# Seven products on the second of four slices, sixteen transfers in place of sixteen ScalarE copies, and weight halves split four ahead

## The chip, the cores and the metric

The kernel runs on one core of a Trainium2 chip. The metric is the device time of one execution in microseconds (us). Of the core's engines, TensorE (PE) multiplies, VectorE (DVE) and ScalarE (ACT) do the elementwise work, and SyncE (SP) issues transfers; each takes its own instructions strictly in order, and they wait for each other by semaphores.

## The reference

Two decoder layers on 256 tokens of width 2048. The change touches only the last two lines of a layer, the SwiGLU part, and what surrounds it:

```python
for l in range(DEPTH):                       # 2 layers
    h = rms_norm(x, attn_norm[l])
    z = h @ w_in[l]                          # 2048 -> 5632, split among three mixers
    ...
    x = x + mix @ w_out[l]                   # 2048 -> 2048
    h = rms_norm(x, ffn_norm[l])
    x = x + (jax.nn.silu(h @ w_gate[l]) * (h @ w_up[l])) @ w_down[l]   # 2048 -> 5632 -> 2048
return rms_norm(x, final_norm)
```

All is float32. The kernel gets float32 accuracy by splitting each operand into a rounded high part and a low remainder and adding three products: high by high, high by low, low by high.

## The kernel before

**Weights.** All weights come as blocks of 512 by 512 (1 MB), in the order of use, into four buffers `wf` (`load_weights`, SP, line 136). Each block is split in two halves (`split_weights`): ACT writes the high part `wh` (line 159), DVE the low part `wl` (line 160); five buffers hold split halves. `ahead(3)`, called at the start of each half's products, splits the half that is used three later. So a half's copy on ACT waits until PE has left the half used five before it.

**Products.** `products` (lines 207 to 209) is six matmuls of 128x512. A plain half is used for both token tiles, twelve matmuls. For one of the four 512-deep slices of gate and up, the one numbered `SEVEN`, the eight products (gate and up, two halves, two token tiles) are replaced by seven on sums (`seven`, `seven_products`): seven singles of six matmuls. In four of the seven, DVE first adds two halves in place (line 154), then ACT copies, then DVE makes the remainder.

**A block f.** Each layer has eleven blocks f of 512 columns of gate and up, in three parts of 4, 4 and 3. In a block PE works through the slices of the 2048-deep sum: first the seven singles of slice 0, then slices 1 to 3, twelve plain halves; 42 + 144 = 186 matmuls. Then DVE and ACT make `mid` = silu(gate) * up (lines 784 to 789). After each part comes its down projection with the `mid` of its blocks, transposed, as the stationary operand: `thd` and `tld`.

**The transposing of a mid.** `block_transposed` puts tasks into a list, and `step()`, called after each half used, runs the next one: DVE transposes 32x32 blocks within partitions (line 434, `btd`); ACT moves the 16 pieces between groups of 32 partitions (line 442, `bod`), four per task; ACT and DVE split the result in two tasks (lines 492 and 493). These seven tasks fall into the uses that follow, which are the seven singles of the next block, or the first halves of the down projection. `later(..., gap=n)` keeps a task at least n steps behind the one before.

**Order.** A scheduler places the instructions on each engine, near the order in which they are written. SP's instructions, loads and others, run in one row, and each transfer uses one of eight completion semaphores in turn, so that the ninth waits for the first to have landed.

Of the kernel before, what the change touches and what calls it, by code (L numbers as in the profile page):

```python
# [11 lines left out]
F32 = mybir.dt.float32  # L12
F32R = mybir.dt.float32r
I32 = mybir.dt.int32
AF = mybir.ActivationFunctionType
ALU = mybir.AluOpType
AX = mybir.AxisListType

P = 128
D = 2048  # L20
S = 256
NT = S // P
L = 2
CW = 512
NX = D // CW
# [28 lines left out]
def trunk_kernel(ctx: ExitStack, tc, x, positions, w_in, gmlp_ln_g, gmlp_ln_b,  # L54
# [8 lines left out]
    nc = tc.nc  # L63
# [9 lines left out]
    def blk(shape, name, dt=F32):  # L73
        return bpool.tile(shape, dt, tag="blk", name=name)
# [7 lines left out]

    PAIR = [(n, k) for n in range(2) for k in range(NX - 1)] + [(n, NX - 1) for n in range(2)]
    PARTS = [list(range(0, 4)), list(range(4, 8)), list(range(8, NF))]
    SEVEN = 0
    wsrc = []
    jobs = []

    def wblock(w, k, c):
        return w[c, k].rearrange("p (k c) -> p k c", k=4)  # L90
# [13 lines left out]
    for l in range(L):  # L104
# [10 lines left out]
        for hv in PARTS:  # L115
            for f in hv:
                for k in range(NX):
                    if k == SEVEN:
                        seven(wblock(w_gate[l], k, f), wblock(w_up[l], k, f))
# [45 lines left out]
    def ahead(n):  # L165

        j = min(state["use"] + n, len(jobs) - 1)
        split_weights(j + 1)
        load_weights(jobs[state["use"]][0] + 4)
# [6 lines left out]
    def later(fn, key=None, wait=0, gap=0):  # L176

        pending.append((fn, key, clock["now"] + wait, gap))
# [13 lines left out]
    def need(key):  # L192
        while key not in done:
            run_one()
# [16 lines left out]
    def block(operand, h, t):  # L211
        return [[x[:, 2 * h + k, t * P:(t + 1) * P] for k in range(2)] for x in operand]

    def weight_tile(acc, operand, first, last):
        for h in range(2):
            ahead(3)
            for t in range(NT):
                products(acc[t], *block(operand, h, t), state["use"], first[t] and h == 0, last and h == 1)
            whalf.pop(state["use"])
            state["use"] += 1  # L220
            step()

    def seven_products(dst, operand, sums):

        sh, sl = sums
        S = [[[x[:, n, k] for k in range(2)] for x in (sh, sl)] for n in range(4)]
        lhs = [block(operand, 0, 0), S[0], S[2], S[3], S[1], block(operand, 1, 0), block(operand, 1, 1)]
        for (acc, first, last), x in zip(dst, lhs):
            ahead(3)
            products(acc, *x, state["use"], first, last)  # L230
            whalf.pop(state["use"])
            state["use"] += 1
            step()
# [57 lines left out]
    stat = {}  # L291
    for c in range(NX):
        xt = blk([P, 4, S], f"xt{c}")
        th, tl = blk([P, 4, S], f"tha0_{c}", F32R), blk([P, 4, S], f"tla0_{c}", F32R)
# [131 lines left out]
    def transpose_later(src, name, per=1, wait=0):  # L426


        b = blk([P, NT, CW], f"bt{name}")
        o = blk([P, 4, S], f"bo{name}")  # L430

        def blocks():
            for t in range(NT):
                nc.vector.transpose(b[:, t], src[:, t])  # L434

        def moves(a0):
            for a in range(a0, a0 + per):
                for q in range(4):
                    s_ = b[32 * a:32 * a + 32].rearrange("p t (k q i) -> p t k q i", k=4, q=4)[:, :, :, q, :]
                    d_ = o[32 * q:32 * q + 32].rearrange("p k (t a i) -> p t k a i", t=NT, a=4)[:, :, :, a, :]  # L440
                    if q < 2 or name.startswith("d_"):
                        nc.scalar.copy(d_, s_)  # L442
                    else:
                        nc.vector.tensor_copy(d_, s_)

        later(blocks, wait=wait)
        for a in range(0, 4, per):
            later(lambda a=a: moves(a))
        return o

    def block_transposed(src, dst, key, gcol, per=1, wait=0):

        nm = "_".join(map(str, key))
        th, tl = blk([P, 4, S], f"th{nm}", F32R), blk([P, 4, S], f"tl{nm}", F32R)
        dst[key] = (th, tl)
        o = transpose_later(src, nm, per=per, wait=wait)
        for h in range(2):
            later(lambda h=h: evac_split(o[:, 2 * h:2 * h + 2], th, tl, 2 * h, gcol), key if h else None)
        return o

    def block_sums(stat, key, gcol):

# [85 lines left out]
    for l in range(L):  # L548
# [193 lines left out]
        stat = {}  # L742
# [3 lines left out]
        def projected(c, acc):  # L746
            add_residual(acc, c)
            norm_chunk(c, ssq, 32 + 16 * l, stat, f"f{l}", c == SEVEN)

# [5 lines left out]
        fkeys = [(f"f{l}", c) for c in range(NX)]  # L755
        rf = None
        for hi, hv in enumerate(PARTS):
            mids = {}
            for f in hv:
                P1, P5, P7, P6 = (trp.tile([P, CW], F32, tag="tr", name=f"p{n}_{f}") for n in (1, 5, 7, 6))  # L760
                C = [[accp.tile([P, CW], F32, tag="acc", name=f"c{f}_{n}{t}") for t in range(NT)] for n in range(2)]
                need(fkeys[SEVEN])
                need((f"f{l}", "sums"))
                alone = (True, True)
                seven_products([(P1, *alone), (P5, *alone), (P7, *alone), (C[1][0], True, False),
                                (P6, *alone), (C[0][0], True, False), (C[0][1], True, False)],
                               stat[fkeys[SEVEN]], stat["sums"])
                if rf is None:
                    rf = token_rstd(ssq, "rf")
                sg, mid = blk([P, NT, CW], "sg"), blk([P, NT, CW], "mid")  # L770

                nc.scalar.copy(sg[:, 0], P1)
                nc.vector.tensor_tensor(mid[:, 0], sg[:, 0], P6, op=ALU.add)
                nc.vector.tensor_tensor(sg[:, 1], mid[:, 0], P7, op=ALU.add)
                nc.vector.tensor_tensor(mid[:, 0], P5, mid[:, 0], op=ALU.subtract)
                nc.vector.tensor_tensor(mid[:, 1], P5, sg[:, 1], op=ALU.subtract)
                rest = [k for k in range(NX) if k != SEVEN]
                for k in rest:
                    need(fkeys[k])
                    for n in range(2):  # L780
                        weight_tile(C[n], stat[fkeys[k]], [False, n == 1 and k == rest[0]], k == rest[-1])
                        for t in range(NT if k == rest[-1] else 0):
                            if n == 0:
                                nc.vector.tensor_tensor(sg[:, t], sg[:, t], C[0][t], op=ALU.add)
                                nc.scalar.activation(sg[:, t], sg[:, t], AF.Silu, scale=rf[:, t:t + 1])
                            else:
                                nc.vector.tensor_tensor(mid[:, t], mid[:, t], C[1][t], op=ALU.add)  # L787
                for t in range(NT):
                    nc.vector.scalar_tensor_tensor(mid[:, t], mid[:, t], rf[:, t:t + 1], sg[:, t],  # L789
                                                   op0=ALU.mult, op1=ALU.mult)  # L790
                block_transposed(mid, mids, ("d", l, f), None)
            lastpart = hi == len(PARTS) - 1
            if lastpart:
                stat2 = {}
                ssq2 = spool.tile([P, NT, NX], F32, tag="ssq", name=f"ssq_n{l}")
                if l == L - 1:
                    fin = [blk([P, 2, CW], f"fin{h}") for h in range(2)]
                    for h in range(2):
                        nc.sync.dma_start(out=fin[h], in_=final_norm[h * 2 * CW:(h + 1) * 2 * CW].rearrange(
                            "(c n) -> c n", c=2).partition_broadcast(P))  # L800
                    xf = [[blk([P, 2, CW], f"xf{t}{h}") for h in range(2)] for t in range(NT)]
            for c in range(NX):
                last = l == L - 1 and lastpart and c == NX - 1
                acc = chunk(mids, [("d", l, f) for f in hv], 2 if last else 0)
                if last:
                    break
                add_residual(acc, c)
                if lastpart:
                    if l + 1 < L:
                        norm_chunk(c, ssq2, 16 * (l + 1), stat2, f"a{l + 1}")  # L810
                    else:
                        sum_squares(c, ssq2)
                        for t in range(NT):
                            nc.gpsimd.tensor_tensor(xf[t][c // 2][:, c % 2], xs[:, t, c * CW:(c + 1) * CW],
                                                    fin[c // 2][:, c % 2], op=ALU.mult)
        stat, ssq = stat2, ssq2
# [3 lines left out]
    ov = out[0].rearrange("(t p) d -> p t d", p=P)  # L820
    c = NX - 1
    for t in range(NT):
# [9 lines left out]
        for h in range(2):  # L832
            o = xf[t][h]
# [47 lines left out]
```

## Time and profile before

| | us |
|---|---|
| median of 3 runs | 2214.27 (2212.69 to 2215.53) |
| profiled execution | 2215.22 |
| its span, first to last instruction | 2213.5 |
| PE busy | 2132.7 (96%) |
| DVE busy | 1594.2 (72%) |
| ACT busy | 1269.1 (57%) |
| 16 DMA engines, mean busy share | 52.4% |

Matmuls overlap in a pipeline, so that a matmul's own duration (389 ns) is not the time that it costs; that is the distance from one start to the next. An engine's idle time counts only where PE, which is busy 96% of the span, is made to wait by it.

### The profile page before, as it was taken

What the parts mean: (1) busy time and instruction counts of PE and PEld (TensorE: products, weight loads), DVE (VectorE), ACT (ScalarE), POOL (GpSimd) and SP (SyncE); (2) the same over time, 40 slices, a digit from 0 to 9 for tenths busy, and PEclk for the clock granted to TensorE, in tenths of its full rate; (3) what the DMA queues carried; (4) which work ended last, traced back from release to release, by engine and by line L of the source; (5) the groups of instructions that cost most, each with busy time, mean ns of one, the idle gap of its engine ahead of it and who ended that gap; (6) DMA issues with size and microseconds to landing.
All of it is one profiled execution on the core that took longest, in us unless ns stands there. A gap on an engine that the chain in (4) does not pass through costs nothing.

```text
span 2213.5 us, 24728 instructions
## 1 busy us (share of the span) xinstructions
PE 2132.7 (96%) x9256; PEld 1736.2 (78%) x9256; DVE 1594.2 (72%) x1970; ACT 1269.1 (57%) x1849; POOL 176.6 (8%) x177
## 2 busy tenths in 40 slices
PE   9999999999999999999999999999899998999898
PEld 7888888777887778877788888887688877888676
DVE  6886788776567765676877768887765777657764
ACT  6565476556445564456756645765663466534663
POOL 6212400000000000000011024000000000000002
PEclk9999999999999999999999999999999999999999
DMA  8654555445554465545554554644465445654463
GB/s 308 226 190 167 195 202 197 171 152 209 191 191 170 152 212 207 190 152 207 177 215 174 193 186 171 220 179 152 170 226 194 171 152 191 219 198 152 165 235 114
DMA packets 62949, 417.44 MB, mean 189 GB/s; under 512 B 7535, under 2 KB 8047, under 8 KB 14189
## 3 DMA queue, kind: packets, MB, share of 16 engines
q1 hardware_dynamic: 62828, 415.86, 52.4%
q8 instruction: 72, 1.18, 0.2%
q14 instruction: 49, 0.39, 0.1%
HBM read 411.65 MB, written 2.10 MB: 187 GB/s over the span
## 4 chain that ended last, share of the span: by engine, by line
PE 77%; DVE 8%; ACT 7%; POOL 4%; issue 3%; DMA 0%; SPq 0%; ACTq 0%; POOLq 0%; DVEq 0%
PE acc L208 14%; PE acc L209 14%; PE acc L207 14%; PE c L207 11%; PE c L208 11%; PE c L209 11%; ACT wh L159 4%; DVE wl L160 3%; ACT bod L442 2%; DVE mid L789 1%; DVE btd L434 1%; DVE mid L787 1%; PE p L208 1%; POOL rtmp L332 1%; PE p L209 1%
## 5 line engine op out<-in xcount | busy, mean ns | idle before, releaser
L160 DVE TENSOR_TENSOR wl<-wf,wh 128x1024 fp32r<-128x1024 f32 (+1 forms) x836 | 1032.7, 1251 | 527.1 <-ACT wh L159 525.4
L159 ACT CAST wh<-wf 128x1024 fp32r<-128x1024 f32 (+1 forms) x836 | 862.6, 1048 | 706.8 <-PE acc L209 350.6
L207 PE MATMUL c<-wh,thf 128*128 128x512 f32 x1144 | 457.8, 400 | 47.3 <-ACT wh L159 47.3
L208 PE MATMUL c<-wl,thf 128*128 128x512 f32 x1144 | 450.6, 394 | 0.6 <-DVE wl L160 0.6
L209 PE MATMUL c<-wh,tlf 128*128 128x512 f32 x1144 | 448.8, 392 | 0.0
L207 PEld LDWEIGHTS c<-wh,thf 128*128 128x128 f32 x1144 | 217.9, 190 | 111.5 <-ACT wh L159 68.2
L207 PE MATMUL acc<-wh,tha 128*128 128x512 f32 x704 | 279.8, 398 | 1.6 <-DVE qm L581 0.7
L208 PE MATMUL acc<-wl,tha 128*128 128x512 f32 x704 | 275.0, 391 | 3.5 <-DVE wl L160 3.5
L207 PE MATMUL acc<-wh,thd 128*128 128x512 f32 x704 | 274.2, 389 | 3.6 <-ACT thd L492 3.6
L209 PE MATMUL acc<-wh,tla 128*128 128x512 f32 x704 | 274.7, 390 | 0.0
L208 PE MATMUL acc<-wl,thd 128*128 128x512 f32 x704 | 274.0, 389 | 0.0
L209 PE MATMUL acc<-wh,tld 128*128 128x512 f32 x704 | 273.6, 389 | 0.0
L208 PEld LDWEIGHTS c<-wl,thf 128*128 128x128 f32 x1144 | 217.2, 190 | 50.0 <-DVE wl L160 3.0
L209 PEld LDWEIGHTS c<-wh,tlf 128*128 128x128 f32 x1144 | 217.1, 190 | 43.9
L442 ACT COPY bod<-btd 32x256 f32<-32x256 f32 x352 | 142.1, 404 | 85.3 <-DVE btd L434 80.9
L208 PEld LDWEIGHTS acc<-wl,tha 128*128 128x128 f32 x704 | 132.2, 188 | 33.2 <-DVE wl L160 6.7
L207 PEld LDWEIGHTS acc<-wh,thd 128*128 128x128 f32 x704 | 132.2, 188 | 31.6 <-ACT thd L492 4.4
L207 PEld LDWEIGHTS acc<-wh,tha 128*128 128x128 f32 x704 | 132.1, 188 | 30.2 <-issue 1.7
L209 PEld LDWEIGHTS acc<-wh,tla 128*128 128x128 f32 x704 | 132.1, 188 | 28.0
L209 PEld LDWEIGHTS acc<-wh,tld 128*128 128x128 f32 x704 | 132.2, 188 | 27.5
L208 PEld LDWEIGHTS acc<-wl,thd 128*128 128x128 f32 x704 | 132.2, 188 | 27.5
L208 PE MATMUL acc<-wl,thm 128*128 128x512 f32 x256 | 99.9, 390 | 0.4 <-DVE wl L160 0.3
(192 smaller groups left out, 1894.5 us busy)
## 6 DMA issues: line engine op xcount, KB each, us to landing
wf<-in_w_gate_dram SPq DMA_DIRECT2D x88, 1024.0 KB, 4.9
wf<-in_w_up_dram SPq DMA_DIRECT2D x88, 1024.0 KB, 4.8
wf<-in_w_down_dram SPq DMA_DIRECT2D x88, 1024.0 KB, 4.8
wf<-in_w_in_dram SPq DMA_DIRECT2D x84, 1024.0 KB, 4.9
wf<-in_w_out_dram SPq DMA_DIRECT2D x32, 1024.0 KB, 4.8
wf<-in_w_in_dram SPq DMA_DIRECT2D x6, 512.0 KB, 6.7
xt<-in_x_t_dram SPq DMA_DIRECT2D x8, 256.0 KB, 6.1
xs<-in_x_dram SPq DMA_DIRECT2D x4, 512.0 KB, 12.6
```

The costliest lines, as they stand in the source:

```text
L159: state["act"] = nc.scalar.copy(wh[:, k:k + w], wf[:, k:k + w])
L160: state["dve"] = nc.vector.tensor_tensor(wl[:, k:k + w], wf[:, k:k + w], wh[:, k:k + w].bitcast(F32), op=ALU.subtract)
L207: nc.tensor.matmul(acc, xh[k], wh[:, k, :], start=first and k == 0, stop=False)
L208: nc.tensor.matmul(acc, xh[k], wl[:, k, :], start=False, stop=False)
L209: nc.tensor.matmul(acc, xl[k], wh[:, k, :], start=False, stop=last and k == 1)
L332: V.tensor_scalar(prod, a, c, None, op0=ALU.mult)
L434: nc.vector.transpose(b[:, t], src[:, t])
L442: nc.scalar.copy(d_, s_)
L787: nc.vector.tensor_tensor(mid[:, t], mid[:, t], C[1][t], op=ALU.add)
L789: nc.vector.scalar_tensor_tensor(mid[:, t], mid[:, t], rf[:, t:t + 1], sg[:, t], op0=ALU.mult, op1=ALU.mult)
```

## The change

Three edits. `SEVEN` becomes 1: a block uses slice 0 as plain halves first (four halves, 48 matmuls), then the seven singles of slice 1, then slices 2 and 3. `ahead(3)` becomes `ahead(4)` in both places. A mid goes through a new function, `moved_transposed`: the same two DVE transposes, written in another layout; then 16 transfers issued by SP, each of 32 partitions by 1 KB; then one task that splits the whole 128x1024 result on ACT and DVE, at least two steps behind the last transfer task.

```diff
-    SEVEN = 0
+    SEVEN = 1
@@ weight_tile, seven_products
-            ahead(3)
+            ahead(4)
@@ transpose_later: moves
-                    if q < 2 or name.startswith("d_"):
+                    if q < 2:
@@
+    def moved_transposed(src, dst, key):
+        th, tl = blk([P, 4, S], f"th{nm}", F32R), blk([P, 4, S], f"tl{nm}", F32R)
+        b = blk([P, 4, 4, NT, 32], f"bt{nm}")
+        o = blk([P, 4, 4 * NT * 32], f"bo{nm}")
...
+        def blocks():
+            for t in range(NT):
+                nc.vector.transpose(b[:, :, :, t].rearrange("p q k i -> p k q i"), src[:, t].rearrange(
+                    "p (k q i) -> p k q i", k=4, q=4))
+        def moves(a):
+            for q in range(4):
+                nc.sync.dma_start(out=o[32 * q:32 * q + 32, a],
+                                  in_=b[32 * a:32 * a + 32, q].rearrange("p k t i -> p (k t i)"))
+        def split():
+            ov = o.rearrange("p a (s i) -> p s a i", i=32)
+            hv, lv = (x.rearrange("p k (t a i) -> p (k t) a i", t=NT, a=4) for x in (th, tl))
+            nc.scalar.copy(hv, ov)
+            nc.vector.tensor_tensor(lv, ov, hv.bitcast(F32), op=ALU.subtract)
+        later(blocks)
+        for a in range(4):
+            later(lambda a=a: moves(a))
+        later(split, key, gap=2)
@@ the blocks f
+                for k in range(SEVEN):
+                    need(fkeys[k])
+                    for n in range(2):
+                        weight_tile(C[n], stat[fkeys[k]], [k == 0] * NT, False)
-                rest = [k for k in range(NX) if k != SEVEN]
+                rest = range(SEVEN + 1, NX)
...
-                block_transposed(mid, mids, ("d", l, f), None)
+                moved_transposed(mid, mids, ("d", l, f))
```

How it moves instructions is shown at one place, the passage from block 4 to block 5 of the first layer; the other passages are alike.

ACT before, from the last but three of block 5's singles: `wh250` to `wh253` are the fourth to seventh of the singles, `wh254` is the first plain half, and `bod`, `thd` belong to the mid of block 4.

```order
L159 CAST wh250_5317<-wf117_5231 128x1024
L442 COPY bod_0_4_5308<-btd_0_4_5307 32x2x4x32 x4
L159 CAST wh251_5332<-wf117_5231 128x1024
L159 CAST wh252_5346<-wf116_5197 128x1024
L442 COPY bod_0_4_5308<-btd_0_4_5307 32x2x4x32 x9
L159 CAST wh253_5363<-wf116_5197 128x1024
L159 CAST wh254_5377<-wf118_5270 128x1024
L442 COPY bod_0_4_5308<-btd_0_4_5307 32x2x4x32 x3
L159 CAST wh255_5391<-wf118_5270 128x1024
L492 CAST thd_0_4_5305<-bod_0_4_5308 128x512
```

ACT after, the same passage: `wh251` to `wh257` are now the seven singles, `wh258` the first half of slice 2.

```order
L159 CAST wh254_5375<-wf119_5315 128x1024
L159 CAST wh255_5396<-wf119_5315 128x1024
L159 CAST wh256_5412<-wf118_5265 128x1024
L482 CAST thd_0_4_5299<-bod_0_4_5302 128x1024
L805 COPY sg_5477<-p1_5_5303 128x512
L159 CAST wh257_5423<-wf118_5265 128x1024
L159 CAST wh258_5437<-wf120_5357 128x1024
```

The 16 copies are gone from ACT's row, and the one split of block 4's mid, which needs all 16 transfers, stands between the sixth and the seventh single.

DVE after, the same passage, from the last of block 4's mid (line 822) to the seventh single:

```order
L822 SCALAR_TENSOR_TENSOR mid_5149<-mid_5149,rf_3268,sg_5148 128x512 x2
L160 TENSOR_TENSOR wl251_5312<-wf118_5265,wh251_5311 128x1024
L471 STREAM_TRANSPOSE btd_0_4_5301<-mid_5149 128x4x4x32 x2
L154 TENSOR_TENSOR wf118_5265<-wf118_5265,wf119_5315 128x1024
L154 TENSOR_TENSOR wf119_5315<-wf119_5315 128x1024
L160 TENSOR_TENSOR wl252_5333<-wf118_5265,wh252_5332 128x1024
...
L154 TENSOR_TENSOR wf118_5265<-wf118_5265,wf119_5315 128x1024
L483 TENSOR_TENSOR tld_0_4_5300<-bod_0_4_5302,thd_0_4_5299 128x1024
L806 TENSOR_TENSOR mid_5478<-sg_5477,p6_5_5306 128x512
L160 TENSOR_TENSOR wl257_5424<-wf118_5265,wh257_5423 128x1024
L160 TENSOR_TENSOR wl258_5438<-wf120_5357,wh258_5437 128x1024
```

On DVE the transposes now stand behind the first single's remainder, and the low part of the mid and line 806, which reads the fifth product, stand ahead of the seventh single's remainder.

SP after: `wf120`, `wf121` are the weights of slice 2 of block 5, `wf122`, `wf123` those of slice 3.

```order
L136 DMA wf120_5357<-in_w_gate_dram 128x2048
L136 DMA wf121_5400<-in_w_up_dram 128x2048
L476 DMA bod_0_4_5302<-btd_0_4_5301 32x256 x16
L136 DMA wf122_5427<-in_w_gate_dram 128x2048
L136 DMA wf123_5488<-in_w_up_dram 128x2048
```

The 16 transfers stand in one row between the loads of slices 2 and 3; before, SP's row held loads alone there.

## Rows read from the trace of the kernel before

**Rows 1.** The page's first part: busy time and share of each engine.

```profile
PE 2132.7 (96%) x9256; PEld 1736.2 (78%) x9256; DVE 1594.2 (72%) x1970; ACT 1269.1 (57%) x1849; POOL 176.6 (8%) x177
```

**Rows 2.** Waits of the whole span, PE: who waited for whom, us, times, longest.

```profile
PE c L207 <- ACT wh L159: 47.3, 54, 2.0
PE p L207 <- ACT wh L159: 14.5, 16, 1.8
...
PE acc L207 <- ACT thd L492: 3.6, 2, 1.8
```

**Rows 3.** Stretches, blocks 4, 5, 6: length, busy by engine (count), PE clock, DMA share, GB/s.

```profile
630.42:673.74 43.32, 42.88 (x188) 34.83 (x186) 32.14 (x32) 21.43 (x22) 0.00 (x0) 1.00 0.53 194
673.74:720.83 47.09, 43.44 (x188) 34.68 (x187) 35.68 (x38) 28.61 (x40) 0.00 (x0) 1.00 0.50 179
720.83:768.95 48.12, 44.78 (x188) 35.70 (x187) 35.77 (x38) 28.70 (x40) 0.00 (x0) 0.96 0.49 175
```

**Rows 4.** The same view of the six stretches of gate and up: their sum.

```profile
sum 1025.40, PE 962.99 PEld 772.66 DVE 760.18 ACT 599.78 POOL 5.44; mean PE 160.50 PEld 128.78 DVE 126.70 ACT 99.96 POOL 0.91
```

**Rows 5.** PE in order of time, us 903 to 910: start, duration, instruction [idle before, releaser].

```profile
903.05 0.39 PE L207 MATMUL p<-wh,thf 128*128 128x512 f32 x1
...
909.85 0.39 PE L207 MATMUL c<-wh,thf 128*128 128x512 f32 x1
```

**Rows 6.** PE in order of time in block 5's first half.

```profile
680.13 0.49 PE L207 MATMUL p<-wh,sh 128*128 128x512 f32 x1 [0.79 <-ACT wh L159]
...
685.90 0.50 PE L207 MATMUL c<-wh,thf 128*128 128x512 f32 x1 [1.97 <-ACT wh L159]
```

**Rows 7.** ACT in order of time in the same stretch.

```profile
677.35 1.66 ACT L442 COPY bod<-btd 32x256 f32<-32x256 f32 x4 [5.03 <-DVE btd L434]
679.03 1.99 ACT L159 CAST wh<-wf 128x1024 fp32r<-128x1024 f32 x2
681.05 3.73 ACT L442 COPY bod<-btd 32x256 f32<-32x256 f32 x9
```

**Rows 8.** DVE in order of time in the same stretch.

```profile
673.50 1.28 DVE L787 TENSOR_TENSOR mid<-mid,c 128x512 f32<-128x512 f32 x2
674.69 1.41 DVE L789 SCALAR_TENSOR_TENSOR mid<-mid,rf,sg 128x512 f32<-128x512 f32 x2
676.02 1.30 DVE L434 STREAM_TRANSPOSE btd<-mid 128x512 f32<-128x512 f32 x2
...
680.11 2.36 DVE L160 TENSOR_TENSOR wl<-wf,wh 128x1024 fp32r<-128x1024 f32 x2 [1.69 <-ACT wh L159]
```

**Rows 9.** Groups of instructions: busy us, mean ns, idle before and its releasers.

```profile
L160 DVE TENSOR_TENSOR wl<-wf,wh 128x1024 fp32r<-128x1024 f32 (+1 forms) x836 | 1032.7, 1251 | 527.1 <-ACT wh L159 525.4
...
L154 DVE TENSOR_TENSOR wf<-wf,wf 128x1024 f32<-128x1024 f32 x66 | 80.1, 1214 | 1.5
```

**Rows 10.** SP in order of time: one of four loads in a row, 128 partitions by 1 KB.

```profile
51.35 0.42 SPq L390 DMA_DIRECT2D lamt<-in_lambda_k_dram  x1
```

**Rows 11.** SP in order of time: transfers from SBUF to SBUF.

```profile
224.57 0.63 SPq L716 DMA_DIRECT2D x<-xh  x1
225.25 0.93 SPq L717 DMA_DIRECT2D x<-xh  x1
...
227.74 0.54 SPq L719 DMA_DIRECT2D x<-xh  x1
```

**Rows 12.** DMA issues: line, count, KB each, median us from issue to landing.

```profile
wf<-in_w_gate_dram SPq DMA_DIRECT2D x88, 1024.0 KB, 4.9
```

**Rows 13.** Transfers that write x (SBUF to SBUF): us to landing.

```profile
DMA to landing us min/median/max: 4.8/5.3/5.4
```

**Rows 14.** Transfers that write the output, 512 KB each: us to landing.

```profile
DMA to landing us min/median/max: 2.7/3.1/3.5
```

**Rows 15.** PE in order of time at the start of a three-block part's down projection.

```profile
1052.91 0.39 PE L208 MATMUL acc<-wl,thd 128*128 128x512 f32 x1
1055.09 0.50 PE L207 MATMUL acc<-wh,thd 128*128 128x512 f32 x1 [1.79 <-ACT thd L492]
```

More of the change, by code (lines that the diff above doesn't have):

```diff
@@ L228, in seven_products @@
         for (acc, first, last), x in zip(dst, lhs):
-            ahead(3)
+            ahead(4)
             products(acc, *x, state["use"], first, last)
@@ L459, in block_transposed @@
         return o
+    def moved_transposed(src, dst, key):
+        nm = "_".join(map(str, key))
+        th, tl = blk([P, 4, S], f"th{nm}", F32R), blk([P, 4, S], f"tl{nm}", F32R)
+        b = blk([P, 4, 4, NT, 32], f"bt{nm}")
+        o = blk([P, 4, 4 * NT * 32], f"bo{nm}")
+        dst[key] = (th, tl)
+        def blocks():
[15 more added lines that the diff above has]
+        later(split, key, gap=2)
     def block_sums(stat, key, gcol):
@@ L764, in trunk_kernel @@
                 alone = (True, True)
-                seven_products([(P1, *alone), (P5, *alone), (P7, *alone), (C[1][0], True, False),
-                                (P6, *alone), (C[0][0], True, False), (C[0][1], True, False)],
+                seven_products([(P1, *alone), (P5, *alone), (P7, *alone), (C[1][0], False, False),
+                                (P6, *alone), (C[0][0], False, False), (C[0][1], False, False)],
                                stat[fkeys[SEVEN]], stat["sums"])
@@ L780, in trunk_kernel @@
                     for n in range(2):
-                        weight_tile(C[n], stat[fkeys[k]], [False, n == 1 and k == rest[0]], k == rest[-1])
+                        weight_tile(C[n], stat[fkeys[k]], [False] * NT, k == rest[-1])
                         for t in range(NT if k == rest[-1] else 0):
```

## The prediction

> **What bounds the kernel now.** I read the page's first part, then PE's waits, then stretches of the timeline, then what stands on each engine in one stretch. PE is busy 96% of the span [rows 1], so only what makes PE wait counts. Its waits are nearly all for `wh`, the high part of a weight half, in the blocks of gate and up: 47.3 + 14.5 us [rows 2]. They cost more than that, since a restart is slow, so I measure the loss against dense work. Where PE never waits, 30 matmuls take 909.85 - 903.05 = 6.80 us, 0.2267 us each [rows 5]. A block's 186 matmuls would take 42.2 us; the 22 blocks, 927.6 us. The six stretches of gate and up last 1025.4 us [rows 4]: 97.8 us are lost there. Block 4, the first of its part, takes 43.3 us and loses 1.1; block 5 takes 47.1 and loses 4.9; block 6, with a PE clock of 0.96 in the row, 48.1 and 5.9 [rows 3]. With 1.2 for each of the six first blocks, the other 16 lose 90.6 us, 5.7 each. The first block has no mid behind it to be transposed; that is the difference to look for.
>
> It stands on ACT in block 5 [rows 7]. ACT idles 5.03 us until the transposes of block 4's mid are done, with the casts for the next singles queued behind. Then come 16 copies (nine of them 3.73 us, so 0.41 each, 6.6 in all) among the casts of 1.0 us. PE runs dry twice, 0.79 and 1.97 us in the rows that I took [rows 6]. DVE meanwhile idles too, 1.69 us for a `wh` [rows 8]: it is ACT that holds all.
>
> One more place waits: at the start of a three-block part's down projection PE stands 1.79 us for the high part of the last mid, two times, 3.6 us [rows 2, 15], nearly 2 each with the restart. So 97.8 + 3.9 = 101.7 us is what the change can win at most, if it adds nothing.
>
> **The change, part by part.** I count from t = 0, where PE starts a block. Plain halves take PE 12 x 0.2267 = 2.72 us, singles 1.36. After the change, four plain halves end at 10.9, and the seven singles S0 to S6 start at 10.9, 12.2, 13.6, 15.0, 16.3, 17.7 and 19.0.
>
> *Copies off ACT.* 16 x 0.41 = 6.6 us go from ACT, and with them the 5.03 us idle, since nothing on ACT now waits for the transposes. Both lay on the path.
>
> *The singles one slice later, one half more ahead.* At t = 0 four halves are split, 10.9 us of work for PE, where three singles were 4.1 us. I follow DVE, the busiest of the two, through its new row. The mid's last adds and products ran from 673.50, 0.24 before the block's start at 673.74, to 676.10 [rows 8], t = 2.4. Then the remainder of S0 (1.18 each where two follow each other [rows 8]), and two transposes, 1.3 [rows 8]: t = 4.9. Two additions, at 1.21 [rows 9]: 7.3. The remainders of S1, S2 and S3: 10.8. The addition for S4: 12.0. ACT's cast, 1.0 [rows 7] and 0.1 of handing over, and its remainder: 14.3; S5: 15.5; the addition for S6: 16.7. Until here each is 1 to 4 us ahead of PE. Then the mid's low part, 1.2 us by the row of a remainder of the same size [rows 9]: 17.9; line 806, 0.64 like an addition of line 787 [rows 8], which needs the fifth product (17.7): 18.5; and S6's remainder: 19.7. PE wants that at its second matmul, 19.0 + 0.23 = 19.3. So about 0.4 us are lost in a block, and the following halves need 1.15 of DVE against 2.72 of PE: the rest stays covered. The limit is now DVE, by little.
>
> *The 16 transfers.* Their time is the open price. ACT's split of the mid stands between the casts of S5 and S6, so if the transfers have landed at T, the mid's parts end at T + 1.1 and T + 2.3, line 806 at T + 3.0, S6's remainder at T + 4.2. The loss in a block is the larger of 0.4 and T - 15.1. SP can start at 4.9. For one issue, the ends are 0.42 us, a load of 128 partitions by 1 KB [rows 10], and 0.93, a transfer from SBUF to SBUF over few partitions [rows 11]; the two between over 112 partitions took 0.54 and 0.63 [rows 11]. I take 0.5 and 0.05 between two, nearer to the short end, because each piece is a plain 1 KB run in 32 partitions. The last then starts at 4.9 + 15 x 0.55 = 13.1 and is issued at 13.6. For landing, the ends are 1.4 and 5.3 us. The upper is a row of 448 KB transfers behind each other [rows 13]. The lower is an estimate: 512 KB take 3.1 [rows 14] and 1 MB takes 4.9 [rows 12], on a straight line 1.4 for 32 KB; the quickest measured is 2.7 [rows 14]. I take 2.1: T = 15.7, a loss of 0.6, and with something for the eight semaphores that ACT and DVE must look at there, 0.8 us a block. With the short ends T is 4.9 + 15 x 0.47 + 0.42 + 1.4 = 13.8 and the loss 0.4; with the long ones 4.9 + 15 x 0.98 + 0.93 + 5.3 = 25.8, and 10.7.
>
> The Trainium skill, DMA: Bandwidth & Descriptors, section "Rules for kernel authors", speaks against such transfers: under 64 KB "you're paying mostly overhead". Its figure of about 2.0 us fixed (same page, "Anatomy of one DMA — SWDGE (gpsimd) path", given for another issuing path) would put landing at 2.1, an estimate, and leave the sum where it is; no row here shows a transfer of 32 KB.
>
> *What is queued behind the transfers.* The next loads on SP are those of slice 3. They need the buffers of the singles' weights, free at 16.7 to 19.7, so the transfers (until 13.6) hold nobody up; PE uses them at 31. On SP's other side, slice 2's loads stand ahead of the transfers and wait for splits done before t = 0. The ninth transfer waits for the first's landing, 4.9 + 0.5 + 2.1 = 7.5, while its own turn comes at 9.3: no cost, unless landing takes over 4.
>
> *Down projections.* The last mid of a part has no block behind it. In a part of four PE wants it at half 7, t = 16.3; in the parts of three the scheduler now puts the next chunk's first halves ahead, to about the same time. With T = 15.7 the high part is there at 16.8: 0.5 to 1.5 us each. I take 1.0 for each of six; before it was 3.9 in all.
>
> *First blocks.* Four of six have no mid and no norm behind them: 0.3 each. A layer's first still has the last norm's tasks beside it: 1.2 as now.
>
> *`ahead(4)` elsewhere.* The other stages are dense already; a gain or a loss of 2 us a layer bounds it. I take nothing.
>
> **The sum.** Before: 101.7. After: 16 x 0.8 + 4 x 0.3 + 2 x 1.2 + 6 x 1.0 = 22.4. Gain 79 us of the profiled execution's 2215.2: 2136. The median of the runs shown, 2214.3, is 0.9 lower: 2135 to 2136.
>
> **Rivals.** *DVE is late all the same.* Each added single is a chain of addition, cast and remainder, and DVE idled 1.69 us in such a chain [rows 8]. The new row has additions in pairs, which fills that; if it doesn't, some 3 us a block stay: 48 + 4 + 12 = 64, gain 38, 2177. Against it: ACT is idle then.
>
> *The transfers are a little late.* T from 18 to 19.5 loses 2.9 to 4.4 a block, and at that size the clock falls in some blocks, 1.0 us as in block 6 against 5 [rows 3]: 16 x 4.3 + 4 + 6 x 4 = 97, gain 5, 2210.
>
> *The transfers become the bound: slower.* At 0.93 an issue and 2.7 to land, T is 23.2 and each block waits 8.1, plus 1.0 of clock; that is 16 x 9.1 + 4 + 6 x 8 = 198, 96 more than now: 2311. It decides from T = 20, where a block loses as much as now. For it: the transfer over 15 partitions, the nearest to 32 from below, took 0.93 to issue [rows 11]. Against it: it stood in a row behind 448 KB, while here the queue is empty, since the last load, issued about t = 0, lands in 4.9 [rows 12].
>
> *The change doesn't do what it says.* ACT could still wait in line, since the mid's split stands in its row; that is the case just priced.
>
> **How the numbers follow.** The forecast, with losses of 0.4 to 2.5 a block and 11 to 60 us in all, 2124 to 2173: 0.62. DVE late: 0.12. Transfers a little late: 0.10, nearly even. Transfers the bound: 0.14. Better than any of these: 0.02. For 8 in 10 the range goes from 2120 to 2205; above it lie the slower case and half of the late one. 0.2%, 4.4 us, is about what a measurement of this kernel can tell from no change. Faster: 0.62 + 0.12 + 0.02 and most of the late case, 0.83; same 0.03; slower 0.14.
>
> **What would show it.** Right: PE's waits for `wh` below 15 us in all; ACT without idle time for the transposes; blocks of 42.5 to 43.5 us; the 16 issues at 0.4 to 0.6 us each, landed by t = 16. Wrong: ACT's mid split (line 482) with idle time released by a DMA, and PE waiting at S6 and at the first half of slice 2 in every block; or DVE's idle time for `wh` in the singles as it was.

## The result, and the profile after

| | us |
|---|---|
| before, median of 4 runs beside it | 2214.72 (2212.69 to 2215.53) |
| after, median of 4 runs | 2151.66 (2151.23 to 2152.01) |
| ratio, 95% interval | 0.9717 (0.970 to 0.9733) |
| profiled execution after, its span | 2151.74, 2150.0 |

Faster by 63 us; 2136 was forecast, with a range of 2120 to 2205. The page's busy line, beside [rows 1]: ACT fell from 1269.1 to 1127.1 and DVE stayed, as it should when 352 copies of 0.40 go from ACT.

```profile
PE 2116.3 (98%) x9256; PEld 1731.5 (81%) x9256; DVE 1592.9 (74%) x1948; ACT 1127.1 (52%) x1475; POOL 175.5 (8%) x177
```

Of the waits (who waits, for whom: us, times, longest), these bear on the change. PE's 47.3 and 14.5 for `wh` in gate and up [rows 2] are down to 8.4. New is ACT's wait for the transfers at line 482, in every one of 22 blocks.

```profile
ACT thd L482 <- DMA bod<-btd: 47.2, 22, 3.1
DVE tld L483 <- ACT thd L482: 20.3, 22, 2.9
...
PE c L207 <- ACT wh L159: 8.4, 23, 0.4
...
PE acc L207 <- ACT thd L482: 7.5, 6, 3.0
```

Blocks 4, 5 and 6 (window, length, busy time of each engine, PE clock), beside [rows 3]: 42.3, 43.9 and 43.2 us where 43.3, 47.1 and 48.1 stood. The sum of the six stretches of gate and up fell from 1025.40 [rows 4] to 950.84.

```profile
619.35:661.67 42.32, 42.32 (x187) 34.83 (x186) 32.14 (x32) 21.21 (x22) 0.00 (x0) 1.00 0.53 199
661.67:705.53 43.86, 43.01 (x187) 34.84 (x186) 35.59 (x37) 22.06 (x23) 0.00 (x0) 1.00 0.57 204
705.53:748.68 43.15, 42.77 (x187) 34.84 (x186) 35.58 (x37) 22.06 (x23) 0.00 (x0) 1.00 0.60 207
```
```profile
sum 950.84, PE 940.50 PEld 766.39 DVE 771.79 ACT 494.97 POOL 3.70; mean PE 156.75 PEld 127.73 DVE 128.63 ACT 82.50 POOL 0.62
```

Block 5 in order of time (start, duration, instruction, idle before), from t = 0 at 661.67; beside [rows 6 to 8]. It is one of five blocks in which a single issue took over 1 us, and so one of the dearer ones. First SP's 16 transfers, with what the profile tells of all 352 (duration of an issue in ns, then the time from the start of an issue to its landing in us):

```profile
666.47 10.76 SPq L476 DMA_DIRECT2D bod<-btd  x16
```
```profile
L476 SPq DMA_DIRECT2D bod<-btd x352: 507/589/1891, 406.1 to 2086.8; - x176
...
DMA to landing us min/median/max: 1.8/1.9/3.9
```

ACT, then DVE, then PE:

```profile
678.64 1.05 ACT L482 CAST thd<-bod 128x1024 fp32r<-128x1024 f32 x1 [2.87 <-DMA bod<-btd]
679.59 0.58 ACT L805 COPY sg<-p 128x512 f32<-128x512 f32 x1
680.07 4.84 ACT L159 CAST wh<-wf 128x1024 fp32r<-128x1024 f32 x5
```
```profile
677.25 1.23 DVE L154 TENSOR_TENSOR wf<-wf,wf 128x1024 f32<-128x1024 f32 x1
679.72 1.22 DVE L483 TENSOR_TENSOR tld<-bod,thd 128x1024 fp32r<-128x1024 f32 x1 [1.25 <-ACT thd L482]
680.86 0.68 DVE L806 TENSOR_TENSOR mid<-sg,p 128x512 f32<-128x512 f32 x1
681.46 3.49 DVE L160 TENSOR_TENSOR wl<-wf,wh 128x1024 fp32r<-128x1024 f32 x3
```
```profile
680.48 0.39 PE L209 MATMUL c<-wh,tlf 128*128 128x512 f32 x1
681.17 0.50 PE L207 MATMUL c<-wh,thf 128*128 128x512 f32 x1 [0.30 <-ACT wh L159]
682.12 0.50 PE L207 MATMUL c<-wh,thf 128*128 128x512 f32 x1 [0.44 <-ACT wh L159]
682.73 0.50 PE L208 MATMUL c<-wl,thf 128*128 128x512 f32 x1
683.07 0.40 PE L209 MATMUL c<-wh,tlf 128*128 128x512 f32 x1
```

ACT's split, released by the transfers, begins at 678.64 (T = 17.0); only then come line 805 and, at 680.07, the cast for S6. Its addition had been ready since 678.5. S6's remainder begins at 681.46. PE starts S6 0.46 late (681.17 - 680.48 - 0.23). The next product in PE's row is already the following half's first, whose cast ends 0.95 after S6's: 0.72 more. Then S6's remainder: 0.39. The product behind it starts 0.34 later, 0.11 more than in dense work.

In ten of the 16 blocks that follow another S6 itself starts on time, and PE waits only behind its first product. So it is in block 6 (t = 0 at 705.53, T = 16.2): the following half's first product starts 0.42 late (725.22 - 724.57 - 0.23), then S6's remainder 0.39.

```profile
721.74 1.05 ACT L482 CAST thd<-bod 128x1024 fp32r<-128x1024 f32 x1 [2.12 <-DMA bod<-btd]
```
```profile
724.57 0.39 PE L207 MATMUL c<-wh,thf 128*128 128x512 f32 x1
725.22 0.50 PE L207 MATMUL c<-wh,thf 128*128 128x512 f32 x1 [0.26 <-ACT wh L159]
```

### The profile page after: what moved, and what is told of

Same layout as the page of the kernel before. It is cut to its first block, busy times and chain, and to the rows that moved or that the text cites. A ratio compares the mean times of both kernels' runs of the same rounds, so it can differ in the third digit from the quotient of the medians.

```text
span 2150.0 us, 24940 instructions
## 1 busy us (share of the span) xinstructions
PE 2116.3 (98%) x9256; PEld 1731.5 (81%) x9256; DVE 1592.9 (74%) x1948; ACT 1127.1 (52%) x1475; POOL 175.5 (8%) x177
## 4 chain that ended last, share of the span: by engine, by line
PE 69%; DVE 9%; SPq 9%; issue 4%; POOL 4%; ACT 3%; DMA 2%; ACTq 0%; POOLq 0%; DVEq 0%
PE acc L209 14%; PE acc L208 13%; PE acc L207 13%; PE c L208 9%; SPq L476 9%; PE c L209 9%; PE c L207 8%; DVE wl L160 4%; DMA bod<-btd 2%; ACT wh L159 1%; DVE btd L471 1%; DVE mid L820 1%; ACT thd L482 1%; DVE mid L822 1%; POOL rtmp L332 1%
## 5 line engine op out<-in xcount | busy, mean ns | idle before, releaser
L207 PE MATMUL c<-wh,thf 128*128 128x512 f32 x1144 | 448.3, 392 | 8.5 <-ACT wh L159 8.4
L209 PEld LDWEIGHTS c<-wh,tlf 128*128 128x128 f32 x1144 | 214.8, 188 | 43.9
L209 PE MATMUL acc<-wh,tlm 128*128 128x512 f32 x256 | 99.7, 390 | 0.0
```

The source lines that it names most:

```text
L207: nc.tensor.matmul(acc, xh[k], wh[:, k, :], start=first and k == 0, stop=False)
L209: nc.tensor.matmul(acc, xl[k], wh[:, k, :], start=False, stop=last and k == 1)
```

## The experiments

The loss of a block below is its length on PE less 186 x 0.2267 = 42.17 us, as a mean of the 16 blocks that follow another in their part; about 0.1 of it is left in every kernel. "Half clock" counts those of the 16 in which matmuls start 0.43 us apart for a while instead of 0.23. Both are read from the one profiled execution of each kernel. Ratios are to the kernel before on the same chip.

| singles in slice, mid moved by, halves ahead | median us | ratio (95%) | loss | half clock |
|---|---|---|---|---|
| first, ACT, 3 (before) | 2214.7 | 1 | 5.64 | 8 |
| second, ACT, 3 (`e_seven_only`) | 2171.2 | 0.9803 (0.9788 to 0.9817) | 2.96 | 0 |
| first, transfers, 3 (`e_moves_only`) | 2194.1 | 0.9903 (0.9887 to 0.992) | 3.80 | 3 |
| first, ACT, 4 (`e_ahead_only`) | 2209.1 | 0.9973 (0.9963 to 0.9982) | 4.94 | 14 |
| second, transfers, 3 (`e_ahead3`) | 2166.1 | 0.9782 (0.9765 to 0.9798) | 2.50 | 4 |
| second, ACT, 4 (`e_copies`) | 2182.1 | 0.9849 (0.9835 to 0.9864) | 3.57 | 6 |
| first, transfers, 4 (`e_seven0`) | 2175.4 | 0.9823 (0.9808 to 0.9837) | 2.63 | 3 |
| second, transfers, 4 (after) | 2151.7 | 0.9717 (0.970 to 0.9733) | 1.23 | 0 |

### One edit alone, and one undone

**The place alone.** `SEVEN = 1` and the order of the slices that goes with it; the rest as before.

> One edit alone: the seven products stand in the second slice; the mid is still turned by 16 copies on ACT, and halves are split three ahead. Theory 1 (the place of the singles and the load of ACT each carry a part of the gain): in a block ACT is free for the copies from t = 4.9, where the transposes end. Ahead of the cast for S4 it then has 16 copies of 0.41, the casts of S1, S2 and S3 (1.05 each), the mid's split in two pieces (1.3) and line 805 (0.9): 6.6 + 3.2 + 1.3 + 0.9 = 12.0, so that cast ends at 18 and its remainder at 19.2, where PE wants it at 16.5. Loss 2.7 a block instead of 5.7 before: 16 x 3.0 = 48 less, about 2167; range 2155 to 2185. Theory 2 (the place alone carries it): 2150 to 2155, as the changed kernel. Theory 3 (freeing ACT carries it): 2205 to 2215.

It took 2171.2 us. In the blocks it is theory 1 (2.96 a block, forecast 2.7): the place alone brings 44 us, where all three edits bring 63, and the copies still cost.

**The transfers alone.** `moved_transposed` in place of `block_transposed`; the rest as before.

> One edit alone: transfers move the mid's blocks; the seven products stay in the first slice, and halves are split three ahead. Theory 1: ACT no longer stands in line, but PE starts the block with three singles, 4.1 us, split, while DVE has the mid's last adds until t = 2.4, the transposes (1.3) and then, for S3 to S6, three additions and four remainders, 8.4: it ends near t = 12, where PE wants S6 at 8.4. Loss 3 to 4 a block, 5.7 before: a gain of 16 x 2.2 = 35, about 2180; range 2160 to 2195. Theory 2 (the place carries it all): 2205 to 2215. Theory 3 (freeing ACT carries it): 2150 to 2160.

It took 2194.1 us and lost 3.80 a block: theory 1 again, at the long end of its range. The transfers alone bring 21 us.

**Four ahead alone**, and **four ahead with the transfers, singles first**:

```diff
-            ahead(3)
+            ahead(4)
```

> The kernel before with halves split four ahead: neither place nor transfers changed. On ACT ten of the 16 copies now stand in one run, 4.1 us, between the casts for two singles, and the rest behind. The first stall of a block (0.95 + 0.72 at t = 6.4) shrinks by part of one single's 1.36; the second (2.1 + 0.72 at 12.2) is ACT's sum of copies and casts, 6.6 + 1.3 + seven casts, and stays: 4 to 5 a block, 2200 to 2212. Rival (the fourth half is worth its 1.36 whatever else is on ACT): 2190 to 2195.

It took 2209.1 us, in the range, but not by that reasoning. In the two blocks where the clock held, a block lost 3.57 instead of 4.9 before, the 1.36 of the rival. In the other 14 the half clock took it back: the two neighbours here (window, ..., PE clock, DMA, GB/s) differ by 1.6 us.

```profile
944.98:992.32 47.34, 44.66 (x188) 35.84 (x187) 35.82 (x38) 28.60 (x40) 0.00 (x0) 0.96 0.49 178
992.32:1038.05 45.73, 43.08 (x188) 34.69 (x186) 33.41 (x36) 28.38 (x40) 0.00 (x0) 1.00 0.56 207
```

> The changed kernel with the seven products first again: transfers and four halves ahead alone. With three ahead (e_moves_only) a block lost 3.25 in two places, 0.46 + 0.72 at t = 5.9, for S3, and 1.13 + 0.72 at 10.7, for the first half behind the singles. With S3 split before the block begins, the first of the two goes; the second, DVE's work for the singles and the mid in a row, stays or shrinks by part of S3's 2.4. Loss 1.0 to 2.0 a block: 16 x 1.75 = 28 less than 2194, 2166; range 2155 to 2180. Rival (the fourth half counts only with the singles in the second slice): 2190 to 2196.

It took 2175.4 us, with a loss of 2.3 where the clock held and 2.63 in the mean. As expected, the first stall went, but for 0.2, and the second stayed, and it stayed whole (1.14 + 0.72); in three blocks the half clock came on top.

**Four ahead undone.** The changed kernel with `ahead(3)` in both places.

> The changed kernel with halves split three ahead instead of four. Theory 1: PE starts a block with 8.2 us of split halves instead of 10.9, and DVE, which is ahead of PE by 1 to 4 us until S5, has room for that; the wait for the mid's split on ACT is as it was. Nothing in the blocks, and the start of the program, where the changed kernel lost about 3 us more than the one before (its first stage and the attention's), gets them back: 2146 to 2154. Theory 2 (the fourth half is a part of the gain): one single's time, 1.36 us, is lost in each of 16 blocks: 2165 to 2180.

It took 2166.1 us, 14 more than after: theory 2 by its time, though the fourth half works in another way. The transfers start 1.1 us sooner here, and still S6 is later. DVE in a block of this kernel:

```profile
946.11 1.23 DVE L483 TENSOR_TENSOR tld<-bod,thd 128x1024 fp32r<-128x1024 f32 x1 [1.51 <-ACT thd L482]
947.26 1.22 DVE L154 TENSOR_TENSOR wf<-wf,wf 128x1024 f32<-128x1024 f32 x1
948.39 0.68 DVE L806 TENSOR_TENSOR mid<-sg,p 128x512 f32<-128x512 f32 x1
949.66 3.50 DVE L160 TENSOR_TENSOR wl<-wf,wh 128x1024 fp32r<-128x1024 f32 x3 [0.59 <-ACT wh L159]
```

The addition for S6 (line 154) stands behind the mid's low part, which waits for the transfers; with four ahead it is written one half sooner and stands ahead of it (677.25 above). That is 1.2 us in the chain; in a quiet block 0.7 is left of it, since the transfers come sooner, and four blocks fall to the half clock. The six stretches of gate and up last 971.04 us for 950.84, 20 more, while the rest of the kernel is 4 shorter than after. The four runs lie between 2163.6 and 2171.3 us at mean granted clocks of 0.997 to 0.993, so how many blocks fall differs from run to run. With three ahead the transfers thus bring only 5 us over `e_seven_only`.

**Transfers undone.** The changed kernel with `block_transposed` for the mid.

> The changed kernel with the 16 copies on ACT instead of the 16 transfers. Theory 1: ACT's row is 12.0 us from the end of the transposes to the cast of S4 (16 copies 6.6, three casts 3.2, the split 1.3, line 805 0.9), one cast less where the fourth half was split before: S4's remainder at 18 to 19 against 16.5. Loss 1.5 to 2.7 a block against 1.2 with transfers: 2157 to 2180. Theory 2 (the transfers' landing costs as much as the copies did, so their only effect is to trade one wait for another): 2148 to 2156.

It took 2182.1 us, just above theory 1's range: the transfers are worth 30 us in this setting. The fourth half, worth 14 us with transfers, costs 11 with copies (2171.2 without). The stalls add up to the same in both, 2.9 a block where the clock held, but they are split differently: 0.9, 0.9 and 0.72 with three ahead, 0.5, 1.37 and 0.72 here. Six blocks here fall to the half clock, none with three ahead: 6 x 1.6. One such stretch, on PE:

```profile
734.51 0.50 PE L207 MATMUL c<-wh,thf 128*128 128x512 f32 x1 [1.21 <-ACT wh L159]
735.46 0.50 PE L207 MATMUL c<-wh,thf 128*128 128x512 f32 x1 [0.45 <-ACT wh L159]
...
736.81 0.63 PE L209 MATMUL c<-wh,tlf 128*128 128x512 f32 x1
737.24 0.63 PE L207 MATMUL c<-wh,thf 128*128 128x512 f32 x1
...
739.79 0.57 PE L208 MATMUL c<-wl,thf 128*128 128x512 f32 x1
740.21 0.39 PE L209 MATMUL c<-wh,tlf 128*128 128x512 f32 x1
```

### What still holds a block up

**The mid's split behind S6.** The transfers are untouched; only the row changes, but for the last mid of a part. `state["act"]` and `state["dve"]` are the latest cast and remainder written; the split goes behind them:

```diff
-            nc.scalar.copy(hv, ov)
-            nc.vector.tensor_tensor(lv, ov, hv.bitcast(F32), op=ALU.subtract)
+            if last:
...
+            with tc.issue_after(state["act"].ins):
+                nc.scalar.copy(hv, ov)
+            with tc.issue_after(state["dve"].ins):
+                nc.vector.tensor_tensor(lv, ov, hv.bitcast(F32), op=ALU.subtract)
```

> The changed kernel, with only the place of the mid's split (lines 482 and 483) moved: on ACT it stands behind the cast for S6 instead of ahead of it, on DVE behind the remainder of S6, except for the last mid of a part. The transfers are as they were. Theory A (what a block still loses, 0.9 to 1.8 us, is S6 waiting on ACT behind the split that waits for the transfers' landing): S6's addition is done at t = 17.05, its cast at 18.15, its remainder at 19.4, where PE wants it at 19.3; a block loses 0.1 to 0.4. 16 blocks win 0.8 to 1.2 each: 2133 to 2140. Theory B (DVE's chain of the singles is late by itself, whatever ACT waits for): blocks go on losing 0.9 or more, 2148 to 2155.

It took 2145.7 us (ratio 0.9682, 0.9668 to 0.9697), with a loss of 0.88: between the two. The singles are on time, as theory A has it, but a new stall of 0.55 stands at t = 21.5. DVE and PE there:

```profile
677.89 1.23 DVE L160 TENSOR_TENSOR wl<-wf,wh 128x1024 fp32r<-128x1024 f32 x1 [1.19 <-ACT wh L159]
679.03 1.22 DVE L489 TENSOR_TENSOR tld<-bod,thd 128x1024 fp32r<-128x1024 f32 x1
680.17 4.63 DVE L160 TENSOR_TENSOR wl<-wf,wh 128x1024 fp32r<-128x1024 f32 x4
```
```profile
680.43 0.62 PE L207 MATMUL c<-wh,thf 128*128 128x512 f32 x2
681.45 0.50 PE L208 MATMUL c<-wl,thf 128*128 128x512 f32 x1 [0.39 <-DVE wl L160]
```

The mid's low part no longer waits for anything; its own 1.2 us, between two remainders that PE wants at once, is the stall. That gave theory C.

**Two halves further back.** As above, with a gap of 4 instead of 2 steps ahead of the split.

> As e_late, with the mid's split two halves further back on both engines: behind the casts and remainders of slice 2's first two halves. In e_late a block lost 0.77, of it 0.55 + 0.11 at t = 21.5, where the remainder of slice 2's first half stood on DVE behind the mid's low part, 1.2 us. Theory C (the loss is the row: whatever stands on DVE between S6 and the next half makes PE wait, since DVE is then level with PE; from the second half on each half leaves DVE 1.5 us free): with two halves more ahead of it, remainders end at 19.4, 20.6, 21.7, the mid's low part at 22.9, the third half's remainder at 24.1, where PE wants it at 26.0. A block loses 0.1 to 0.2: 16 x 0.6 = 10 less than e_late, 2134 to 2138. Rival (one of ACT and DVE is late in any case after the singles, and the stall only moves to the third half): 2143 to 2147.

It took 2133.9 us (0.9633, 0.9619 to 0.9647), as theory C has it: a block loses 0.20 in the mean, most lose 0.13. Blocks 5 and 6 (second and third line) are as long as block 4 (first line), which has no mid of a block before it to take up, and DVE does 35.5 us in each all the same:

```profile
615.77:658.07 42.30, 42.30 (x188) 34.84 (x186) 32.14 (x32) 21.19 (x22) 0.00 (x0) 1.00 0.54 199
658.07:700.37 42.30, 42.30 (x188) 34.84 (x186) 35.49 (x37) 21.96 (x23) 0.00 (x0) 1.00 0.58 212
700.37:742.67 42.30, 42.30 (x188) 34.84 (x186) 35.49 (x37) 21.95 (x23) 0.00 (x0) 1.00 0.59 211
```

**Half of the transfers issued from ACT.**

```diff
-                nc.sync.dma_start(out=o[32 * q:32 * q + 32, a],
+                (nc.sync if q % 2 else nc.scalar).dma_start(out=o[32 * q:32 * q + 32, a],
```

> The changed kernel with 8 of the 16 transfers issued from ACT, the other 8 from SP; the mid's split stays where it was, between the casts for S5 and S6. SP alone needs 4.8 + 8 x 0.633 = 9.9 for its share, ACT has 8 issues of some 0.6 and the casts of S1 to S3 from t = 4.8, 4.8 + 4.8 + 3.2 = 12.8. Theory A: T falls from 16.2 to 14.5 or so, S6's remainder to 18.7, and a block loses 0.1 to 0.5; the down projections' first waits, 1.3 to 1.6 each, shrink too: 16 x 0.9 + 6 = 20 less, 2130 to 2140; if an issue costs ACT much more than 0.6, its casts for S2 and S3 are late and it gives 2150 or more. Theory B: blocks as in the changed kernel, only the down projections win: 2144 to 2150.

It took 2154.5 us (0.9728, 0.9712 to 0.9745), no gain. The split starts at t = 14.5, the time forecast, but not because the transfers land then: in a quiet block they are all issued by 11.0 and have landed by 12.2, and the split's turn in ACT's row comes after the casts for S4 and S5. A block lost 1.69, more than after. Theory A's formula fell here. ACT no longer waits at line 482; it waits for S6's addition. ACT in block 6 (t = 0 at 706.90):

```profile
715.89 1.99 ACTq L476 DMA_DIRECT2D bod<-btd  x3
...
721.43 1.04 ACT L482 CAST thd<-bod 128x1024 fp32r<-128x1024 f32 x1
...
725.35 4.84 ACT L159 CAST wh<-wf 128x1024 fp32r<-128x1024 f32 x5 [2.40 <-DVE wf L154]
```

The scheduler has put the mid's low part and lines 806 and 807 ahead of S6 on DVE, with S6's addition among them:

```profile
722.88 1.22 DVE L483 TENSOR_TENSOR tld<-bod,thd 128x1024 fp32r<-128x1024 f32 x1
724.02 1.22 DVE L154 TENSOR_TENSOR wf<-wf,wf 128x1024 f32<-128x1024 f32 x1
725.15 0.68 DVE L806 TENSOR_TENSOR mid<-sg,p 128x512 f32<-128x512 f32 x1
725.87 0.69 DVE L807 TENSOR_TENSOR sg<-mid,p 128x512 f32<-128x512 f32 x1
726.47 4.63 DVE L160 TENSOR_TENSOR wl<-wf,wh 128x1024 fp32r<-128x1024 f32 x4
```

So this is no test of faster transfers in an unchanged row; what they would win there no run shows. The down projections did win: five of six start without a wait. The Trainium skill (Trainium Kernel Development and Optimization, "Key Constraints") says that issuing from several engines saves the sequencer's issue time alone; the trace agrees, the 16 issues took 6.2 us for 10.0 in a quiet block and the median landing stayed at 1.9.

**Transfers twice as many, half as large.**

> The changed kernel with 32 transfers of 16 KB for 16 of 32 KB. If an issue costs 0.59 whatever its size, the last lands at T = 4.8 + 32 x 0.633 + 1.4 = 26.5 instead of 16.2. In the row of ACT the split then stands behind the casts for slice 2's first four halves, no longer ahead of S6. Theory A (the loss is the place of the wait in ACT's row, not how long the transfers take): the blocks, with transfers twice as slow, lose less than in the changed kernel, 0.1 to 0.4 instead of 0.9 to 1.8, 13 us less; the last mid of a part has nothing to hide behind, and each of the six down projections starts some 10 to 12 us late: 2152 - 13 + 66 = 2205, 2190 to 2215. Rival (PE waits for the transfers as such): 10 us more in each of 16 blocks and 6 starts, above 2330. If an issue is by its bytes, T stays near 16 to 18 and the time at 2140 to 2160.

It took 2197.0 us (0.9915, 0.990 to 0.993): the time as expected, its parts not. In the singles nothing is lost but 0.1 to 0.5 although the transfers land at 26 to 28: that part of the theory holds. But a block loses 2.08, nearly all of it at slice 3. SP and ACT there:

```profile
717.53 21.53 SPq L477 DMA_DIRECT2D bod<-btd  x32
739.18 0.51 SPq L136 DMA_DIRECT2D wf<-in_w_gate_dram  x1
```
```profile
740.40 1.05 ACT L483 CAST thd<-bod 128x1024 fp32r<-128x1024 f32 x1 [5.91 <-DMA bod<-btd]
...
744.30 1.99 ACT L159 CAST wh<-wf 128x1024 fp32r<-128x1024 f32 x2 [2.37 <-DMA wf<-in_w_gate_dram]
```

The weights of slice 3 are queued on SP behind 32 issues and land after the mid's split is done; the expectation had left that queue out. PE loses 45 us in the down projections, 12.3 after.

**All together.** The split as in `e_late`, four ahead in gate and up and three elsewhere, and for the last mid of a part half of the issues from ACT; then the same with the split as in `e_later`.

> Three things together, each meant for one remaining loss of the changed kernel: the mid's split behind S6 (as in e_late), halves split four ahead in the blocks of gate and up alone and three ahead elsewhere, and for the last mid of a part 8 of the 16 transfers issued from ACT. By theory A: 16 blocks win 0.8 to 1.2, the first chunk of each of six down projections 1 us, the projection after attention 1 us (it lost 1.0 three ahead and 2.2 four ahead): 2152 - 16 - 6 - 1 = 2129, range 2124 to 2136. By theory B only the last two terms: 2145.

The first took 2134.0 us (0.9628, 0.9613 to 0.9642): in the range, but not by its parts. The blocks won 6 us for 16, since the stall of `e_late` is here as well, and the down projections 11 for 6.

> As e_best, with the mid's split behind slice 2's first two halves as in e_later. Theory C: 16 x 0.6 = 10 less than e_best, 2124, range 2121 to 2127. Rival: 2132 to 2136.

The second took 2121.2 us (0.9575, 0.9561 to 0.959), as theory C has it, and is the fastest, 30 us below after. PE loses 1.6 us in all in the down projections, and it is busy 99%:

```profile
PE 2102.5 (99%) x9256; PEld 1731.6 (82%) x9256; DVE 1589.8 (75%) x1948; ACT 1123.8 (53%) x1475; POOL 175.8 (8%) x177
```

## Where the prediction was right, and where it was not

| term | forecast | measured |
|---|---|---|
| 16 blocks that follow another | 12.8 | 19.8 |
| 6 first blocks | 3.6 | 3.4 |
| 6 starts of down projections | 6.0 | 12.3 |
| elsewhere | 0 | 2.7 |
| gain of the profiled execution, 101.7 less these | 79 | 63.5 |

- **What bound the kernel, and the two causes: right.** They were ACT in line for the transposes and copies, and the little cover for the singles. Alone, the place brings 44 us and the transfers 21; undone from the changed kernel, the transfers are worth 30 and the place 24. The gains do not add: place and transfers with three ahead bring 49.
- **The signs: most right.** PE's wait for `wh` is 8.4 (below 15), blocks that follow another take 43.1 to 44.05 us (42.5 to 43.5), ACT no longer waits for the transposes, and the transfers release its split at 16.2 at best (16). The sign set down for wrong is there at a small size: ACT waits at line 482 in every block, and so does PE at the first half of slice 2, while S6 itself starts late in six of the 16.
- **T mis-sized: the main miss, and part of it hidden by luck.** The step took 0.5 an issue and 0.05 between; it is 0.589 and 0.633 from start to start, and in five of 16 blocks one issue takes 1.0 to 1.5. The first issue came at 4.8, as worked out, so the 16 are issued at 14.8 in a quiet block, for 13.6. Landing made up for some of that. The sum put 2.1 behind the end of the last issue, though [rows 12 to 14] count from the start of an issue, so that it counted the issue twice. From its start a transfer lands in 1.9, and the split starts 1.4 after the last issue's end. T is 16.2 in a quiet block and up to 17.1, for 15.7.
- **The formula, T - 15.1: right for this row alone.** It gives 1.1 at 16.2 and 1.9 at 17.0; measured 0.9 and 1.7. `e_act` and `e_ahead3` break it, since S6's addition stands elsewhere in DVE's row.
- **"The limit is now DVE", 0.4 at S6: never the larger of the two.** T set the loss in every block. The 0.4 followed from the mid's low part and line 806 standing ahead of S6, so it was the row and not the amount of work: with the mid's parts behind the next slice's halves (`e_later`) most blocks lose 0.13, and DVE does the same work.
- **"A restart is slow": wrong but for 0.11.** That much the product after a stall costs (682.73 to 683.07). The 0.72 that follows the stalls in block 5 is the row: the next half's first product, whose cast ends 0.95 later, less one matmul.
- **`ahead(4)`: a reason missed in the blocks, a small cost elsewhere.** In the blocks the fourth half was counted as cover. It is worth 20 us there, but by the place of S6's addition in DVE's row and by the clock that held (`e_ahead3`). Elsewhere the prediction took nothing, within 2 us a layer, and 2.7 are lost: in the projection behind attention PE loses 2.2 to 2.7 with four ahead in every kernel, 0.9 to 1.2 with three, so 1.3 come from there. Most of the rest lies in the first stage, in a stretch at half clock 50 us after the start, which some kernels with three ahead have as well. What brings it there stays open.
- **Down projections: low by half.** Five starts lose 1.4 to 1.6, for 1.0, by the same T. The sixth, where the 16 issues took 11.3 us for 10.0, lost 4.9, of it over 1 by the half clock.
- **Rivals.** The transfers a little late is what is left, at a third of its price (1.23 a block for 2.9 to 4.4). DVE late all the same is refuted by `e_later`. The slower case needed 0.93 an issue in the mean; some issues are that long, but not all.

## What to carry to other kernels

Engines take their rows in order: in block 5 the cast for S6 stood 1.6 us behind a split that waited, with its own addition ready. Where a new wait is put on an engine, look at what stands behind it, and place the waiting instruction where its engine has time to spare. Here two halves later was worth 18 us. An edit that only changes how far ahead work is written can change the order on another engine, and its worth depends on the other edits; test it both alone and with them. Two small stalls close together can cost half the clock for a while on top of their own time, 1.6 us each time in `e_copies`.

## What the hardware showed

- A transfer of 32 partitions by 1 KB within SBUF takes SP 0.589 us to issue and lands 1.9 after the issue's start; at half the size the issue is as long (32 in 20.1 us in a quiet block) and landing 1.8. Some single issues take 1.0 to 1.9 us. The Trainium skill (DMA: Bandwidth & Descriptors, "Rules for kernel authors") calls such transfers mostly overhead, and this bears it out; but with their issues off PE's path they were still 30 us cheaper in all than 6.6 us of ACT a block on it (`e_copies`).
- In `e_copies` two stalls, 1.37 and 0.72 with one product between them, are followed by matmuls 0.43 apart (granted clock 0.51 from 736.81 to 740.21 in the lines above, so 1.2 in place of 2.4 GHz) in six of 16 blocks, and by none in the other ten with the same stalls. Stalls of 0.9 and 0.72 in `e_seven_only` were never followed by it, those of 1.14 and 0.72 in `e_seven0` in three of 16 blocks. Each such stretch cost 1.6 us. Why it comes in one block and not in the next stays open.
